# Loading the last third of an image batch in transfers of 16 strided rows

## The chip, the cores and the metric

The kernel runs on one core of a Trainium2 chip. The time is device time in microseconds, the median over runs of the whole kernel; the span of a profile is a little shorter, because it goes from the first to the last instruction. The core's data movers are 16 DMA engines, which work through queues of transfers. "DVE" is VectorE, the engine that does the copies here; "SP" is SyncE, which only issues transfers, and "SPq" is its queue of issued instructions.

## The reference

```python
batch, c, h, w = 32, 3, 256, 256
x = np.random.randn(batch, c, h, w).astype(np.float32)

def reference(x):
    return np.rot90(x, k=2, axes=(-2, -1)).astype(np.float32)
```

Each of the 96 images of 256 x 256 numbers is turned by 180 degrees. Seen as one flat run of 65536 numbers, an image is simply reversed. 25.17 MB are read and 25.17 MB are written.

## The kernel before

The 96 images are worked on in three groups of 32. In a group every image is cut into four strips of E = 16384 numbers, so a group is a tile of 128 rows with 64 KB in each row. All three tiles (A, Bt, Ct) stand in the on-chip memory (SBUF) at once. A group is loaded, VectorE reverses every row in place, and the store writes the four strips of each image in reversed order.

```python
G = 32
E = L // 4            # 16384 numbers, 64 KB
J = E // 8            # 2048
x4 = x.rearrange("b c h w -> (b c) (h w)").rearrange(
    "(g n) (s e) -> g (n s) e", n=G, s=4)
o4 = out.rearrange("b c h w -> (b c) (h w)").rearrange(
    "(g n) (s e) -> g n s e", n=G, s=4)
# ... tiles A, Bt, Ct of 128 x E and T of 128 x J; copy() and back() left out

def load(t, g, lo, hi, queue=nc.sync):
    return queue.dma_start(out=t[:, lo:hi], in_=x4[g][:, lo:hi])

def store(t, g, lo, hi):
    return nc.sync.dma_start(out=o4[g][:, ::-1, lo:hi], in_=t[:, lo:hi])

def inside(t):        # twelve copies: reverse each row in place, through T
    for lo in range(0, E // 2, J):
        hi = E - lo - J
        copy(T[:, :], back(t, hi, hi + J))
        copy(t[:, hi:hi + J], back(t, lo, lo + J))
        copy(t[:, lo:lo + J], T[:, :])

TAIL = 1536
HEAD = 512
load(A, 0, 0, HEAD, nc.scalar)
load(A, 0, HEAD, E)
load(Bt, 1, 0, E)
body = load(Ct, 2, 0, E - TAIL)
load(Ct, 2, E - TAIL, E)
inside(A)
LEAD = 128
store(A, 0, 0, LEAD)
first = store(A, 0, LEAD, E)
tc.add_manual_dep(first.ins, body.ins.name, ...,
    reason="the first store is queued while the last strip is on its way")
for g, t in ((1, Bt), (2, Ct)):
    inside(t)
    store(t, g, 0, E)
```

The third tile comes in two transfers of 128 rows: the first 58 KB of every row (`body`), then the last 6 KB of every row. The large first store is made to wait for `body`: it is issued while the 6 KB pieces are still on their way.

Of the kernel before, what the change touches and what calls it, by code (L numbers as in the profile page):

```python
# [2 lines left out]

os.environ.setdefault("NEURON_RT_ULTRASERVER_MODE", "4")

# [4 lines left out]


@with_exitstack
def kernel(
    ctx: ExitStack,
    tc: tile.TileContext,
    x: bass.AP,
    out: bass.AP,
):

    nc = tc.nc
    P = 128

    B, C, H, W = x.shape
    L = H * W
    G = 32
    E = L // 4
    J = E // 8
# [6 lines that stand above are left out]
    pool = ctx.enter_context(tc.tile_pool(name="slots", bufs=1))  # L42
    A = pool.tile([P, E], x.dtype, tag="A")
    Bt = pool.tile([P, E], x.dtype, tag="B")
    Ct = pool.tile([P, E], x.dtype, tag="C")
    T = pool.tile([P, J], x.dtype, tag="T")

    def back(t, lo, hi):
        return t[:, hi - 1:(lo - 1 if lo else None):-1]

    def copy(dst, src):
        tc.keep_in_program_order(nc.vector.tensor_copy(out=dst, in_=src))  # L52

    def load(t, g, lo, hi, queue=nc.sync):
        return queue.dma_start(out=t[:, lo:hi], in_=x4[g][:, lo:hi])  # L55

    def store(t, g, lo, hi):
        return nc.sync.dma_start(
            out=o4[g][:, ::-1, lo:hi], in_=t[:, lo:hi])

    def inside(t):
# [3 lines that stand above are left out]
            copy(t[:, hi:hi + J], back(t, lo, lo + J))  # L65
            copy(t[:, lo:lo + J], T[:, :])

    TAIL = 1536
    HEAD = 512
    load(A, 0, 0, HEAD, nc.scalar)  # L70
    load(A, 0, HEAD, E)
    load(Bt, 1, 0, E)
    body = load(Ct, 2, 0, E - TAIL)
    load(Ct, 2, E - TAIL, E)
    inside(A)
    LEAD = 128
    store(A, 0, 0, LEAD)
    first = store(A, 0, LEAD, E)
    tc.add_manual_dep(
        first.ins, body.ins.name,  # L80
        mybir.DependencyInfo(mybir.DependencyClass.Sync, mybir.DependencyReason.DATA),
# [6 lines that stand above are left out]
# [1 line left out]
_INS = ['x']  # L89
_OUTS = [((32, 3, 256, 256), 'float32')]  # L90


# [23 lines left out]
```

## Time and profile before

| | |
|---|---|
| time, median of 3 runs | 122.06 us (121.93 to 122.1) |
| span of the profiled run | 120.2 us |
| VectorE busy | 44.2 us, 36 copies of 1.23 us |
| DMA packets on the main queue | 1152, 50.07 MB |
| load of A (its large part), issue to landing | 21.9 us |
| load of Bt, issue to landing | 40.8 us |
| two loads of Ct, issue to landing | 57.9 and 59.3 us |
| store of Bt and of Ct, issue to landing | 39.8 and 42.7 us |

A page of the profile begins with the busy time of each engine. Register, semaphore and DMA-issuing instructions do not count as busy. DMA work has its own lines: packets, bytes, and the share of the 16 engines' span that the packets took. The time from issue to landing includes the time that a transfer stands behind others in its queue. A wait is told as who waited, for whom, the total, the number of times and the longest.

### The profile page before, as it was taken

To read this page: it belongs to the slowest core of one execution; us is meant where nothing else is said; L and a number is where in the kernel's file an instruction comes from. 1 tells how busy PE (TensorE), PEld (TensorE's weight loads), DVE (VectorE), ACT (ScalarE), POOL (GpSimd) and SP (SyncE) were. 2 spreads that over 40 slices of the span, in tenths; PEclk is the share of its full clock that TensorE was granted. 3 is DMA by queue.
4 is the path that set the end of the run, shared out by engine and by line. 5 is a ranking of instruction groups with operands and counts; after the bars stand their busy time and mean duration, and the time that the engine had idled before them with its cause. 6 is when DMAs were issued, how large, how long until landed. Compare 5 with 4: busy or idle time off the path is not lost.

```text
span 120.2 us, 97 instructions
## 1 busy us (share of the span) xinstructions
DVE 44.2 (37%) x36; POOL 0.2 (0%) x4
## 2 busy tenths in 40 slices
DVE  0000000499995099999059999500000000000000
POOL 0000000000000000000000000000000000000000
DMA  9888988899889879979499777988898889888990
GB/s 338 349 349 349 698 349 349 360 654 393 349 349 633 382 316 553 395 316 633 178 452 693 346 346 346 693 349 349 349 698 349 349 349 698 349 349 349 654 393 0
DMA packets 1296, 50.33 MB, mean 419 GB/s; under 512 B 144, under 2 KB 272, under 8 KB 528
## 3 DMA queue, kind: packets, MB, share of 16 engines
q1 hardware_dynamic: 1152, 50.07, 97.0%
q10 hardware_dynamic: 144, 0.26, 0.6%
HBM read 25.17 MB, written 25.17 MB: 419 GB/s over the span
## 4 chain that ended last, share of the span: by engine, by line
DMA 34%; DVE 25%; another core or an unknown queue 4%; issue 1%; SPq 0%; DVEq 0%
DMA Bt<-in_x_dram 34%; DVE T L52 8%; DVE Bt L52 8%; DVE Ct L52 8%; SPq L55 0%; DVEq L52 0%
## 5 line engine op out<-in xcount | busy, mean ns | idle before, releaser
L52 DVE COPY T<-A 128x2048 f32<-128x2048 f32 x4 | 4.9, 1226 | 22.7 <-DMA A<-in_x_dram 22.6
L52 DVE COPY T<-Ct 128x2048 f32<-128x2048 f32 x4 | 4.9, 1227 | 4.5 <-DMA Ct<-in_x_dram 4.4
L52 DVE COPY T<-Bt 128x2048 f32<-128x2048 f32 x4 | 4.9, 1226 | 4.4 <-DMA Bt<-in_x_dram 4.3
L52 DVE COPY Bt<-Bt 128x2048 f32<-128x2048 f32 x4 | 4.9, 1227 | 0.1
L52 DVE COPY A<-A 128x2048 f32<-128x2048 f32 x4 | 4.9, 1227 | 0.1
L52 DVE COPY A<-T 128x2048 f32<-128x2048 f32 x4 | 4.9, 1227 | 0.1
L52 DVE COPY Bt<-T 128x2048 f32<-128x2048 f32 x4 | 4.9, 1227 | 0.1
L52 DVE COPY Ct<-T 128x2048 f32<-128x2048 f32 x4 | 4.9, 1227 | 0.1
L52 DVE COPY Ct<-Ct 128x2048 f32<-128x2048 f32 x4 | 4.9, 1227 | 0.1
L100 POOL MEMSET const-bfloat16-1.0<- 128x1 bf16 x1 | 0.1, 101 | 0.0
L100 POOL MEMSET const-uint8-127<- 128x1 uint8 x1 | 0.1, 101 | 0.0
L100 POOL MEMSET const-float32-0.0<- 128x1 f32 x1 | 0.1, 98 | 0.2 <-issue 0.2
L100 POOL MEMSET const-float32-1.0<- 128x1 f32 x1 | 0.1, 98 | 0.0
## 6 DMA issues: line engine op xcount, KB each, us to landing
out_dram<-A SPq DMA_DIRECT2D x1, 8128.0 KB, 21.1
A<-in_x_dram SPq DMA_DIRECT2D x1, 7936.0 KB, 21.9
Ct<-in_x_dram SPq DMA_DIRECT2D x1, 7424.0 KB, 57.9
Ct<-in_x_dram SPq DMA_DIRECT2D x1, 768.0 KB, 59.3
A<-in_x_dram ACTq DMA_DIRECT2D x1, 256.0 KB, 22.0
out_dram<-A SPq DMA_DIRECT2D x1, 64.0 KB, 35.2
Bt<-in_x_dram SPq DMA_DIRECT2D x1, 40.8
out_dram<-Bt SPq DMA_DIRECT2D x1, 39.8
```

Of the source, the lines that this page charges most:

```text
L52: tc.keep_in_program_order(nc.vector.tensor_copy(out=dst, in_=src))
L100: nc = _bacc.Bacc("TRN2", target_bir_lowering=False, num_devices=1)
```

## The change

The third group is loaded row by row in place of column by column. A transfer takes rows b, b+8, b+16, ..., b+120: sixteen rows of 64 KB. For b = 0 to 6 the rows are whole; for b = 7 they come as the first 16 KB and then the last 48 KB. `body`, for which the first store waits, is now the 16 KB part of the eighth transfer. When it has landed, 48 KB for each of 16 rows are still on their way, as many bytes as in the 6 KB pieces of 128 rows before. The aim is to have fewer and larger pieces of rows, and to leave a single piece per row of the last transfer as the cover for the first store. All loads are also kept in the order in which they stand in the program.

```diff
     def load(t, g, lo, hi, queue=nc.sync):
-        return queue.dma_start(out=t[:, lo:hi], in_=x4[g][:, lo:hi])
+        return tc.keep_in_program_order(
+            queue.dma_start(out=t[:, lo:hi], in_=x4[g][:, lo:hi]))
@@
-    TAIL = 1536
+    TAIL = 12288
+    R = 8
     HEAD = 512
     load(A, 0, 0, HEAD, nc.scalar)
     load(A, 0, HEAD, E)
     load(Bt, 1, 0, E)
-    body = load(Ct, 2, 0, E - TAIL)
-    load(Ct, 2, E - TAIL, E)
+
+    def rows(t, g, b, lo, hi):
+        return tc.keep_in_program_order(nc.sync.dma_start(
+            out=t[b::R, lo:hi], in_=x4[g][b::R, lo:hi]))
+
+    for b in range(R - 1):
+        rows(Ct, 2, b, 0, E)
+    body = rows(Ct, 2, R - 1, 0, E - TAIL)
+    rows(Ct, 2, R - 1, E - TAIL, E)
     inside(A)
     LEAD = 128
     store(A, 0, 0, LEAD)
```

## The prediction

> **What bounds the kernel now.** I read the page's parts 1 to 4 first, then who waited for whom (compute and the DMA queue's own), then a table of busy time in stretches cut at the landings, last the DMA view of one stretch.
>
> ```profile
> DVE 44.2 (37%) x36; POOL 0.2 (0%) x4
> ...
> q1 hardware_dynamic: 1152, 50.07, 97.0%
> ...
> HBM read 25.17 MB, written 25.17 MB: 419 GB/s over the span
> ```
> VectorE works in 37% of the span; the 16 DMA engines have something in hand in 97% of theirs. Every byte is read once and written once, so no byte can be saved: only the rate can change.
>
> ```profile
> DVE T L52 <- DMA A<-in_x_dram: 22.6, 1, 22.6
> DVE T L52 <- DMA Ct<-in_x_dram: 4.4, 1, 4.4
> DVE T L52 <- DMA Bt<-in_x_dram: 4.3, 1, 4.3
> ...
> SPq L58 <- DMA Ct<-in_x_dram: 33.1, 2, 32.5
> ```
> VectorE waits for each of the three loads, so the loads never wait for it. The last line is the wait that the change edits: the queue holds the large first store until the body of the third group has landed.
>
> ```profile
> 22.62 1.23 DVE L52 COPY T<-A 128x2048 f32<-128x2048 f32 x1 [22.62 <-DMA A<-in_x_dram]
> ...
> 42.05 1.23 DVE L52 COPY T<-Bt 128x2048 f32<-128x2048 f32 x1 [4.33 <-DMA Bt<-in_x_dram]
> ...
> 60.27 0.55 SPq L58 DMA_DIRECT2D out_dram<-Bt  x1
> 61.55 1.23 DVE L52 COPY T<-Ct 128x2048 f32<-128x2048 f32 x1 [4.40 <-DMA Ct<-in_x_dram]
> ...
> 76.68 0.54 SPq L58 DMA_DIRECT2D out_dram<-Ct  x1
> ```
> These are rows of the timeline: start, duration, engine. The copies that start a group mark the landings. Group 2 takes 42.05 - 22.62 = 19.43 us, group 3 takes 61.55 - 42.05 = 19.50 us, for 8192 KB = 8.389 MB each: 432 and 430 GB/s, or 27 GB/s for each of 16 engines. A row is 64 KB and an engine carries 8 rows of a group, so a row costs 19.43/8 = 2.43 us.
>
> ```profile
> 42.00:61.50 19.50, 14.72 (x12) 0.00 (x0) 1.00 1.03 438
> 61.50:81.00 19.50, 14.72 (x12) 0.00 (x0) 1.00 0.99 427
> 81.00:100.00 19.00, 0.00 (x0) 0.00 (x0) 1.00 1.02 442
> ```
> Columns: stretch, length, VectorE, GpSimd, clock, DMA share, GB/s. The rate is flat across the turn from loads to stores at 61.5 us. There is no hole at the turn that a better overlap could close.
>
> ```profile
> DMA  0099000980089000990089000990089000499999
> GB/s 0 0 975 975 0 0 0 1584 365 0 0 365 1584 0 0 0 1462 487 0 0 365 1584 0 0 0 1462 487 0 0 365 1584 0 0 0 202 441 403 418 1318 1100
> ```
> This is group 3's stretch, 42.0 to 61.5 us, in slices of 0.49 us. A packet is counted when it ends. A burst comes every five slices, 2.4 us, and lasts about two: the 16 engines finish their rows within about a microsecond of each other. They work in step. From slice 35 on the short 6 KB ends of the rows fill the picture evenly.
>
> [...]
>
> **The change part by part.** Group 3 now arrives as seven transfers of rows b, b+8, ..., b+120 and an eighth in two column parts. Bytes are the same.
>
> 1. Small packets go. Before, each engine carries 8 rows in two pieces, so 8 packets more than with whole rows. Group 3 cost 19.50 us against 19.43 for group 2: these 8 packets are worth 0.07 us. After, an engine has 9 data packets (7 whole, 16 KB, 48 KB), so about 0.06 us comes back.
> 2. Completion messages are added: nine transfers in place of two, seven more completions per engine. The page counts 144 packets under 512 B for 9 transfers, so 7 x 16 = 112 more. If each costs what a cut costs, 0.07/8 = 0.009 us, that is 0.06 us per engine: points 1 and 2 cancel.
> 3. Issuing: the two group-3 loads took 1.01 us of the queue from 1.63 us on, about 0.5 us each. Seven more are 3.5 us, done by about 6.2 us; the DMA engines reach group 3 at 42 us. Nothing.
> 4. The first store's cover. Before, 6 KB x 8 = 48 KB per engine remain when the body has landed; after, 48 KB of one row remain. At 2.43 us per 64 KB both are 1.82 us. The queue issues at 59.6 us, after the body, and the stores follow without a hole. Same cover, no change.
> 5. The ports. [...] All engines go through b in the same order and in step, so at any moment of this load two engines stand at one port[...]. If a port carries what one engine carries, 27 GB/s, a row takes 2 x 2.43 = 4.86 us, and group 3 takes 8 x 4.86 = 38.9 us in place of 19.5: plus 19.4 us. This lies wholly on the path: the stores stand behind these rows in the same engine queues, and VectorE has no other work to offer.
> 6. Given back: an engine that starts its rows a little ahead of its partner has the port alone for that time, and again at the change from b = 3 to b = 4. With engines in step within a microsecond I allow 0.4 us for that.
> 7. VectorE: its work on group 3 starts at about 42 + 38.9 = 81 us and takes 15.1 us (61.55 to 76.68), so ends at 96. The stores of groups 1 and 2 keep the engines till about 81 + 2 x 19.3 = 120, so the third store is queued in time. With half rate the 48 KB cover 3.6 us. Neither binds.
>
> Sum: 122.06 + 19.4 - 0.4 = 141.1 us, with points 1 to 4 at zero.
>
> **The rivals.** (a) The ports do not bind here. Then only points 1 to 4 count and the time is 122.0 to 122.2 us. For it: the trace before cannot tell an engine's limit of 27 GB/s from a port's, and a kernel tuned this far was presumably given this change for a reason. [...] (b) The engines fall out of step. If one of two partners gets the port first each time, it is through b = 0 to 3 at full speed while the other stands; then it goes to the free ports and the other catches up. Group 3 then takes three half groups, 29.2 us, plus 9.7: 131.8 us. Against it: the bursts above show no engine running ahead over 61 us. (c) The HBM pitch binds instead: 16 rows 512 KB apart in place of rows 64 KB apart inside an engine. [...] (d) The 16 rows of a transfer are given to engines by row number, not one each. [...] the time is as in (a). The even count of completions speaks against it only weakly. (e) The queue is late: with many transfers in flight it may have to wait for an early landing before a later issue. It has from 2 to 42 us for it and each further row is 2.4 us of cover, so I give it nothing.
>
> **Range and chances.** I give about three in four to the port mechanism at or near its full size, 138 to 142.5 us; about 8% to partial loss of step, 131 to 138; about 15% to (a), (c) or (d), near 122; the rest to something worse than half rate. A range of 131 to 143 holds the first two. Faster by over 2% would need more than 2.4 us from a kernel whose DMA engines are busy for 97%: 0.02. Within 2%: 0.14. Slower: 0.84.
>
> **What would show it.** Right: the copy that starts group 3 begins near 80.5 us, not 61.5; the stretch from 42 us to it runs at about 215 GB/s with DMA share still near one, since packets take longer and engines do not idle; the bursts come every ten slices' worth, 4.9 us; group 2's landing stays at 42 us and the stores keep 430 GB/s. Rival (b) shows 320 GB/s for a while and full rate in the middle. Wrong altogether: group 3 at 430 GB/s, and the start of its copies still at 61.5 us. A hole between the last load and the first store would show point 4 wrong.

## The result and the profile after

The changed kernel takes 143.44 us (median of 5 runs, 143.19 to 143.55) against 122.04 us for the kernel before beside it: the ratio is 1.175, with a 95% interval of 1.174 to 1.177. The change costs 21.4 us.

The page of the changed kernel, parts 1 and 3:

```profile
DVE 44.2 (31%) x36; POOL 0.2 (0%) x4
...
q1 hardware_dynamic: 1152, 50.07, 97.2%
...
HBM read 25.17 MB, written 25.17 MB: 356 GB/s over the span
```

VectorE does the same 44.2 us of work, and the DMA queue moves the same bytes in the same number of packets (112 fewer pieces of data, 112 more messages of completion). Its share of the engines' time is still 97%, although only 356 GB/s go through in place of 419. So the busy share cannot show this loss: a packet of 64 KB that takes 5.11 us in place of 2.42 counts as busy all the while.

The timeline of the changed kernel, from the landing of group 1 on:

```profile
22.76 1.23 DVE L52 COPY T<-A 128x2048 f32<-128x2048 f32 x1 [22.76 <-DMA A<-in_x_dram]
...
42.66 1.23 DVE L52 COPY T<-Bt 128x2048 f32<-128x2048 f32 x1 [4.80 <-DMA Bt<-in_x_dram]
...
80.21 0.55 SPq L59 DMA_DIRECT2D out_dram<-Bt  x1
83.28 1.23 DVE L52 COPY T<-Ct 128x2048 f32<-128x2048 f32 x1 [25.52 <-DMA out_dram<-A]
...
98.40 0.54 SPq L59 DMA_DIRECT2D out_dram<-Ct  x1
```

Group 3 lands 83.28 - 42.66 = 40.62 us after group 2, in place of 19.50. That is 21.1 us of the 21.4. Group 2 itself lands 0.61 us later than before (42.66 against 42.05); 0.14 us of that is already there when group 1 lands (22.76 against 22.62). The brackets name a store of A as what ended VectorE's wait, but the copy reads Ct. The chain of waits names the right one:

```profile
47.74 35.26 DMA Ct<-in_x_dram
83.00 0.03 DVEq L52
```

The last piece of Ct landed at 47.74 + 35.26 = 83.00 us. The small store of A landed 0.2 us after it (issued at 52.92, 30.3 us to its landing), and the wait was put down to the later of the two.

Stretches of the changed kernel, in the columns of before: the load of group 3, then two stretches of stores.

```profile
42.70:81.00 38.30, 14.68 (x12) 0.00 (x0) 1.00 0.93 192
83.30:102.00 18.70, 14.70 (x12) 0.00 (x0) 1.00 1.03 446
102.60:121.50 18.90, 0.00 (x0) 0.00 (x0) 1.00 1.02 444
```

The stores are as fast as ever. Only the load of group 3 is slow, at less than half rate. From landing to landing it is 8.389 MB / 40.62 us = 207 GB/s; the 192 is lower because packets are counted when they end.

The DMA view from 42.0 to 61.5 us, in slices of 0.49 us as before:

```profile
DMA  0000000999000000069960000000999000000069
GB/s 0 0 0 0 0 0 0 941 672 538 0 0 0 0 0 0 0 134 1076 807 134 0 0 0 0 0 0 0 941 672 538 0 0 0 0 0 0 0 134 1076
```

The bursts now come every ten to eleven slices, 5.1 us, and still all 16 engines are in one burst: each row takes over twice as long (5.11 us in the median, against 2.42 in group 2 of the same run), and the engines stay in step.

The rest of the page gives no second cause. The queue did have to wait before it could issue some of the row transfers, each time for an earlier landing:

```profile
SPq L77 <- DMA Bt<-in_x_dram: 18.5, 1, 18.5
SPq L77 <- DMA A<-in_x_dram: 18.2, 1, 18.2
...
SPq L77 <- DMA Ct<-in_x_dram: 4.6, 1, 4.6
```

But the last of them was issued by 48.3 us, soon after the first row of group 3 had landed, with most of six rows and the 16 KB piece of each engine still ahead of it, so no engine ran dry.

### The profile page after: what moved, and what is told of

The parts are those of the page before. It is cut to its first block, busy times and chain, and to the rows that moved or that the text cites. A ratio compares the mean times of both kernels' runs of the same rounds, so it can differ in the third digit from the quotient of the medians.

```text
span 141.5 us, 109 instructions
## 1 busy us (share of the span) xinstructions
DVE 44.2 (31%) x36; POOL 0.2 (0%) x4
## 3 DMA queue, kind: packets, MB, share of 16 engines
q1 hardware_dynamic: 1152, 50.07, 97.2%
## 4 chain that ended last, share of the span: by engine, by line
DMA 57%; DVE 10%; SPq 1%; issue 0%; DVEq 0%
DMA Ct<-in_x_dram 57%; DVE Ct L52 7%; DVE T L52 4%; SPq L56 1%; DVEq L52 0%
## 5 line engine op out<-in xcount | busy, mean ns | idle before, releaser
L52 DVE COPY T<-Ct 128x2048 f32<-128x2048 f32 x4 | 4.9, 1227 | 25.6 <-DMA out_dram<-A 25.5
## 6 DMA issues: line engine op xcount, KB each, us to landing
out_dram<-A SPq DMA_DIRECT2D x1, 64.0 KB, 30.3
```

## The experiments

Theory P says that two engines which write into one SBUF port share its rate. "Port" is here only a name for whatever the engines share at SBUF: no trace shows a port itself, and which rows lie at one port was assumed; the runs test it by their times. What the runs measure is how long a row takes: 2.42 us in the kernel before, 5.11 us in the changed one. Rival T says that a transfer with few rows per engine is slow in itself. Rival H says that rows 512 KB apart in HBM are slow to read. The table gathers all runs; "group 3" is the time from the copy that starts group 2 to the copy that starts group 3 in each timeline, and each diff is against the changed kernel. From e5 on the diffs show only the lines that are put in.

| run | time, us | ratio to before (95%) | group 3, us |
|---|---|---|---|
| before | 122.04 | | 19.50 |
| changed | 143.44 | 1.174 to 1.177 | 40.62 |
| e1, 16 neighbouring rows | 178.08 (one run) | | 74.03 |
| e2, HBM rows neighbouring | 143.21 | 1.169 to 1.176 | 40.26 |
| e3, 128 rows by columns | 122.60 | 1.003 to 1.005 | 19.98 |
| e4, 32 rows, every fourth | 122.18 | 1.000 to 1.002 | 19.46 |
| e5, halves in turn | 141.44 | 1.156 to 1.161 | 38.86 |
| e6, engines one row apart | 126.17 | 1.030 to 1.037 | 23.69 |
| e7, a store in 16-row transfers | 143.81 | 1.177 to 1.181 | 19.46 |
| e8, halves one after the other | 142.95 | 1.170 to 1.174 | 40.37 |
| e9, changed, other order | 141.89 | 1.162 to 1.165 | 39.43 |
| e10, rows two apart | 143.28 | 1.173 to 1.177 | 40.41 |
| e11, as e1, other order | 179.92 | 1.472 to 1.478 | 75.66 |
| e12, 32 neighbouring rows | 144.24 | 1.179 to 1.183 | 40.47 |

**e1: sixteen neighbouring rows.**

```diff
-            out=t[b::R, lo:hi], in_=x4[g][b::R, lo:hi]))
+            out=t[16 * b:16 * b + 16, lo:hi], in_=x4[g][16 * b:16 * b + 16, lo:hi]))
```

> Sixteen neighbouring rows per transfer in place of every eighth row, all else as changed. Theory P (SBUF ports are shared; a port shared by two engines gives 65.5 KB x 2 in 5.1 us, 25.6 GB/s): [...] a row takes about 10.2 us, group 3 about 82 us, and the kernel 122.0 + 82 - 19.4 = 184 to 185 us. Rival T (a transfer with one row per engine is slow in itself, whatever the rows): no change from the changed kernel, 143 us. Rival H (the HBM pitch of 512 KB makes it slow): the pitch is 64 KB now, so near 122 us.

Its timeline:

```profile
44.05 1.23 DVE L52 COPY T<-Bt 128x2048 f32<-128x2048 f32 x1 [6.08 <-DMA Bt<-in_x_dram]
118.08 1.23 DVE L52 COPY T<-Ct 128x2048 f32<-128x2048 f32 x1 [58.92 <-DMA out_dram<-A]
```

Group 3 takes 74.0 us, 9.25 us a row, or 3.8 times the 2.42 us of a single one. T and H fall: the transfers have the same number and size, the HBM pitch is smaller, and the time grows by 35 us. P has the direction and most of the size, but the row was expected at 10.2 us. If four engines share a port here, as the factor of 3.8 suggests, they get more out of it than two do in the changed kernel: 4 x 65.5 KB / 9.25 us = 28.3 GB/s against 25.6. A part of that comes from the order of the transfers, as e11 will show.

**e2: HBM rows apart from SBUF rows.** The rows of group 3 come out in another order; bytes and work are the same.

```diff
-            out=t[b::R, lo:hi], in_=x4[g][b::R, lo:hi]))
+            out=t[b::R, lo:hi], in_=x4[g][16 * b:16 * b + 16, lo:hi]))
```

> SBUF rows as in the changed kernel (every eighth), but each transfer reads 16 neighbouring rows of HBM; the rows of group 3 come out in another order, with the same bytes and the same work. Theory P: the same as the changed kernel, 143.4 us. Rival H whole: 122 us. Rival H for the part by which a shared row (5.115 us) is longer than two single ones (4.84 us): rows fall to 4.84 us and the kernel to about 141.3 us.

Its timeline:

```profile
42.48 1.23 DVE L52 COPY T<-Bt 128x2048 f32<-128x2048 f32 x1 [4.69 <-DMA Bt<-in_x_dram]
...
82.74 1.23 DVE L52 COPY T<-Ct 128x2048 f32<-128x2048 f32 x1 [25.15 <-DMA out_dram<-A]
```

143.21 us: the rows read from HBM are not the cause, not even of the part above twice a single row. At most it holds 0.05 us a row (40.62 - 40.26 over 8).

**e3: as many transfers, all rows in each.**

```diff
-    for b in range(R - 1):
-        rows(Ct, 2, b, 0, E)
-    body = rows(Ct, 2, R - 1, 0, E - TAIL)
-    rows(Ct, 2, R - 1, E - TAIL, E)
+    W = E // R
+    for b in range(R - 1):
+        load(Ct, 2, b * W, (b + 1) * W)
+    body = load(Ct, 2, (R - 1) * W, E - 1536)
+    load(Ct, 2, E - 1536, E)
```

> Nine transfers with nine completions as in the changed kernel, but of 128 rows and 8 KB columns (the last as 2 KB and 6 KB). Theory P: each engine has its own port, so full rate; only 56 more packets per engine at 0.009 us, 0.5 us: 122.5 us. Rival T in the form that the number of transfers and completions costs: 143 us.

122.60 us, as P expected. Nine transfers with nine completions cost next to nothing. 56 more data packets and 7 more completions per engine are worth 0.56 us together, 0.009 us each on average.

**e4 and e12: the same transfers, other rows.** Both use four transfers of 32 rows, the last in two column parts. e4:

```diff
-    TAIL = 12288
-    R = 8
+    TAIL = 6144
+    R = 4
```

e12 has these two lines and also:

```diff
-            out=t[b::R, lo:hi], in_=x4[g][b::R, lo:hi]))
+            out=t[32 * b:32 * b + 32, lo:hi], in_=x4[g][32 * b:32 * b + 32, lo:hi]))
```

> Four transfers of 32 rows (every fourth row), the last with 40 KB and 24 KB columns, so that again 48 KB per engine cover the first store. [...] Theory P with rows dealt by port: each engine has a port of its own, 122.0 us. Theory P with neighbouring rows of a transfer dealt to the same engine: two engines at one port at each step, 143 us. Rival T (cost per transfer): half as many transfers, about 132 us.

> The run with 32-row transfers again (every fourth row: 122.2 us), but each transfer takes 32 neighbouring rows; number, size and pieces of the transfers are the same. Theory P: [...] 143.3 us, as the changed kernel. Rival T (few rows per engine and transfer is what costs): 122.2 us, as with every fourth row.

The timeline of e4:

```profile
42.17 1.23 DVE L52 COPY T<-Bt 128x2048 f32<-128x2048 f32 x1 [4.45 <-DMA Bt<-in_x_dram]
...
61.63 1.23 DVE L52 COPY T<-Ct 128x2048 f32<-128x2048 f32 x1 [4.36 <-DMA Ct<-in_x_dram]
```

The timeline of e12:

```profile
43.72 1.23 DVE L52 COPY T<-Bt 128x2048 f32<-128x2048 f32 x1 [5.38 <-DMA Bt<-in_x_dram]
...
84.19 1.23 DVE L52 COPY T<-Ct 128x2048 f32<-128x2048 f32 x1 [25.38 <-DMA Ct<-in_x_dram]
```

This is the cleanest pair of the study. Number, size and pieces of the transfers are equal; only the rows differ (in HBM too, but in e2 this was worth at most 0.05 us a row). Every fourth row takes 19.46 us, neighbouring rows take 40.47 us. Which rows of SBUF a transfer names decides, not how many. e4 also says something of how the rows are dealt: its rows take 19.46 / 8 = 2.43 us each, so by theory P its 16 engines stand at different ports at each step. Had neighbours in the transfer gone to one engine, the same theory gave 143 us. e12 is 0.9 us above its expectation; its group 2 lands late, at 43.72 us.

**e5 and e6: engines set apart.** Both take every fourth row of one half of SBUF at a time. In e5 all 16 engines are meant to work in one half, then all in the other:

```diff
+    def part(h, r, i0, i1, lo=0, hi=E):
+        a, z = 64 * h + r + 4 * i0, 64 * h + r + 4 * (i1 - 1) + 1
+        return tc.keep_in_program_order(nc.sync.dma_start(
+            out=Ct[a:z:4, lo:hi], in_=x4[2][a:z:4, lo:hi]))
+    for n in range(7):
+        part(n % 2, n // 2, 0, 16)
+    body = part(1, 3, 0, 16, 0, E - TAIL)
+    part(1, 3, 0, 16, E - TAIL, E)
```

e6 gives eight engines a row in advance, so that they are meant to work in one half while the other eight work in the other:

```diff
+    part(1, 3, 0, 8)
+    for n in range(6):
+        part(n % 2, n // 2, 0, 16)
+    body = part(0, 3, 0, 16, 0, E - TAIL)
+    part(0, 3, 0, 16, E - TAIL, E)
+    part(1, 3, 8, 16)
```

> Transfers of 16 rows again, every fourth row of one half of SBUF (rows 0 to 63 or 64 to 127), the halves in turn; HBM pitch 256 KB. [...] Theory P with engines in step: every row is shared as in the changed kernel. At each turn to the other ports an engine that is ahead finds a free port; the changed kernel has one such turn and its row there took 4.88 us in place of 5.115 us, here there are seven turns, so six more times 0.24 us come back: 143.4 - 1.4 = 142.0 us. Rival T: 143.4 us.

> As the run with halves in turn, but an 8-row transfer goes first, which only 8 of the engines take part in, so they are one row ahead and always stand in the other half's ports than their partners; the second 8 rows come last, on the same 8 engines, so these carry 9 rows and the others 7. Theory P: no port is ever shared, a row takes 2.42 us, and the time is that of the kernel before plus one row of imbalance, 122.0 + 2.4 = 124.5 us. If the 8 engines are not those that share ports with the other 8 or the row order differs: 133 to 143 us. Rival T (transfers with one row per engine are slow in themselves): 144 us or more.

The landings of group 2 and group 3 in e5, then in e6:

```profile
42.16 1.23 DVE L52 COPY T<-Bt 128x2048 f32<-128x2048 f32 x1 [4.48 <-DMA Bt<-in_x_dram]
...
81.02 1.23 DVE L52 COPY T<-Ct 128x2048 f32<-128x2048 f32 x1 [23.76 <-DMA out_dram<-A]
```

```profile
42.45 1.23 DVE L52 COPY T<-Bt 128x2048 f32<-128x2048 f32 x1 [4.72 <-DMA Bt<-in_x_dram]
...
66.14 1.23 DVE L52 COPY T<-Ct 128x2048 f32<-128x2048 f32 x1 [8.59 <-DMA out_dram<-A]
```

With half-SBUF transfers as in e5, one row of offset takes 15.3 us away (141.44 to 126.17). Transfers with at most one row per engine ran at close to full rate here, 2.63 to 2.68 us a row in the trace in place of 4.84 in e5, and this ends rival T. Group 3 takes 23.69 us, nine rows of 2.63 us, which fits eight engines that carry nine rows. e6 is 1.7 us above its expectation, since a row takes 2.63 to 2.68 us and not 2.42. What costs a quarter microsecond per row where by theory P no port should be shared wasn't settled; the two sets of engines change sides at about the same time and may overlap there, but that is not shown.

**e7: does it hold for reads of SBUF?** The loads are those of the kernel before, and only the store of group 2 is cut into rows:

```diff
+        if g == 1:
+            for b in range(R):
+                tc.keep_in_program_order(nc.sync.dma_start(
+                    out=o4[g][b // 4::2, 3 - b % 4, :], in_=t[b::R, :]))
+        else:
+            store(t, g, 0, E)
```

> All loads as in the kernel before; the store of group 2 in eight transfers of 16 rows (every eighth). Theory P, if ports bind reads of SBUF as they bind writes: the store of group 2 takes about 40.7 us in place of 19.3, 143.4 us. If ports bind only writes into SBUF: 122.0 us.

Its stretches: the store of group 1, then group 2 in two stretches.

```profile
61.50:81.00 19.50, 14.72 (x12) 0.00 (x0) 1.00 1.12 427
81.00:100.50 19.50, 0.00 (x0) 0.00 (x0) 1.00 0.84 175
100.50:122.00 21.50, 0.00 (x0) 0.00 (x0) 1.00 1.00 235
```

143.81 us. A store from sixteen rows eight apart costs 21.8 us, as the load into such rows does, with nothing changed on the load side. That a shared port is the cause here too is the author's estimate and has no run of its own: these stores also write rows 512 KB apart in HBM, and e2 has tested only reads of HBM.

**e8 to e11: why a shared row is more than twice a single one.** A single row takes 2.42 us in the trace, so a shared one should take 4.84. The changed kernel's rows take 5.11 us, but e5's rows take 4.84. In steady state only one whole row of the changed kernel is shorter, b = 4 with 4.88 us (against 5.11); that fits rows b = 0 to 3 at one set of ports and b = 4 to 7 at another, with a turn between them, but no trace shows the sets. e5 differs in two ways: in the rows that move together (its pairs), and in that every transfer goes to the other half of SBUF than the one before (its turns). These runs part the two. e8 is e5 in another order, e9 the changed kernel in another order, e11 is e1 in another order, and e10 has another step. The four edits, written here as one:

```diff
+    def part(a, step, lo=0, hi=E):        # sixteen rows a, a + step, ...
+        z = a + 15 * step + 1
+        return tc.keep_in_program_order(nc.sync.dma_start(
+            out=Ct[a:z:step, lo:hi], in_=x4[2][a:z:step, lo:hi]))
+    order = (0, 1, 2, 3, 64, 65, 66, 67)         # e8,  step 4
+    order = (0, 4, 1, 5, 2, 6, 3, 7)             # e9,  step 8
+    order = (0, 1, 32, 33, 64, 65, 96, 97)       # e10, step 2
+    order = (0, 32, 16, 48, 64, 96, 80, 112)     # e11, step 1
+    for a in order[:-1]:
+        part(a, step)
+    body = part(order[-1], step, 0, E - TAIL)
+    part(order[-1], step, E - TAIL, E)
```

> The transfers of the run with halves in turn, in another order: all four of the lower half, then all four of the upper. Open is why a row on a shared port takes 5.115 us in the changed kernel and 4.84 us, twice a single row, with halves in turn. Theory Turn (a row is only 2 x 2.42 us when the engine's row before went to other ports, else 0.27 us more): one turn is left of seven, 143.3 us, rows of 5.11 us but the fifth. Theory Pair (it depends on which engines and which rows share a port): pairs as with halves in turn, 141.4 us, rows of 4.84 us.

> The changed kernel's transfers in the order b = 0, 4, 1, 5, 2, 6, 3, 7, so that each row goes to other ports than the one before. Theory Turn: rows of 4.84 us, 141.4 us. Theory Pair: pairs as in the changed kernel, rows of 5.11 us, 143.4 us.

> Sixteen rows two apart: [...] lower half first, then the upper, so one turn. Theory Turn: as the changed kernel, 143.4 us. Theory Pair, in the form that near rows share better (four near rows got 28.3 GB/s out of a port with 16 neighbouring rows, two far ones 25.6): rows of 4.63 to 4.84 us, 139.7 to 141.4 us.

> Sixteen neighbouring rows, [...]. Theory Turn: every second row is longer by 0.27 us or more than the 9.27 us measured there, by 4 x 0.27 = 1.1 us in all or more: 179.2 us or more. Theory Pair: 178.1 us as there.

All four come out on the side of Turn. e8 loses what e5 had gained, with e5's pairs: 142.95 us. e9 gains with the changed kernel's pairs: 141.89 us, though 0.5 us less than expected: its rows take 4.9 us and not 4.84, and why is open. e10, with rows two apart, is not faster: 143.28 us. e11 is 1.8 us over e1 (179.92 against 178.08). The durations of packets in the traces say how (medians; the words on ports are theory P's):

| packet | changed | e9 |
|---|---|---|
| row on the same ports as the row before | 5.11 us | none |
| row after a turn to other ports | 4.88 us | 4.89 to 4.91 us |
| 16 KB of the last row | 1.28 us (no turn) | 1.11 us (turn) |
| 48 KB that follow on the same port | 3.84 us | 3.80 us |

3.84 us for 48 KB is 5.12 us for 64 KB, and the pieces of 40 KB (3.20 us) and 24 KB (1.92 us) in e12 give the same: the excess grows with the bytes, so it is a rate and not a fee per row. Two engines that share get 2 x 65.5 KB / 5.115 us = 25.6 GB/s together, where one alone gets 65.5 KB / 2.418 us = 27.1. A turn gives back 0.2 us in these two runs and 0.27 us in e5, and the 16 KB pieces show most of it at the start of the row. That partners cross at slightly different moments, so that each is alone at its port for a while, fits this but was only argued.

One more reading would be that certain pairs of engines share a path, whatever the rows. Against it: in the kernel before and in e4 all 16 engines work at once, and group 3 takes 19.50 and 19.46 us, 2.43 to 2.44 us a row; the same engines take 40.47 us in e12, where only the rows differ.

## Why the prediction was right and where it was wrong

- **Points 1 and 2, small packets and completions: right.** e3 measures the two together at 0.009 us each, the size taken from the cut of group 3, and e4 lands within 0.2% of before.
- **Point 3, issuing: right in effect.** Issuing was not done by 6.2 us but by 48.3 us, for the queue waited, as rival (e) feared; still the rows were queued in time.
- **Point 4, the cover: right in effect.** The 48 KB did not take 1.82 us but 3.84, the rate of rows of 5.11 us (point 7 has this). The queue had finished with the first store by 80.21 us, 2.8 us before the last of group 3 landed, and the stores run at 444 to 446 GB/s.
- **Point 5, the ports: right that two engines share, wrong in size.** The sharing was the author's estimate, which no trace before had shown; the rows of 5.11 us, e12 against e4 and the offset of e6 fit it. The step that failed is the sentence "If a port carries what one engine carries, 27 GB/s". Two engines that shared moved 25.6 GB/s together. A row is 5.11 us in place of 4.86, eight rows are 2.0 us more, and that is most of the 2.3 us by which 143.44 exceeds 141.1.
- **Point 6, given back: about right.** The first row took 4.70 us in the median and the row after the turn 4.88, together 0.65 us below steady rows; 0.4 was allowed. Against it stands a cost that the sum didn't have: group 2 lands 0.61 us late. 0.14 us of this comes before any row of group 3 is loaded. For the rest the record of packets shows that the data of group 2 end at 41.71 us, 0.15 us later than before, but the last message of completion lands at 42.57 against 41.96. That engines which have already begun group 3 stand at ports where late engines still write group 2 would explain it, and is argued; in e1, with rows of 9.25 us in group 3, the last packet of group 2 took 2.92 us in place of 2.42, and group 2 lands at 44.05 us. With both, 141.1 + 2.0 - 0.25 + 0.6 = 143.45 us. That this meets 143.44 so closely is luck: group 3 took 40.62 us where the terms give 38.9 + 2.0 - 0.65 = 40.25, and what follows its landing is 0.43 us shorter than before (58.22 us of the span against 58.65).
- **Point 7: right.** Neither VectorE nor the cover binds: the third store is issued at 98.40 us, while the engines carry the first.
- **The rivals.** (a), (c) and (d) are out by e12 against e4, by e2, and by the changed kernel itself. (b) did not happen by itself: the bursts stay together. e6 shows what it is worth when it is forced.
- **The range** ended at 143.0 and missed by 0.44 us. It left room below for engines out of step, and almost none above, though the trace before held nothing on how two engines share a port. With half of the 430 GB/s of before, 215, taken as certain for group 3, the sum had no term for the difference to the 207 GB/s measured.

## What to carry to other kernels

A DMA transfer is not described by its bytes and its count of rows: which rows of SBUF move at the same moment decides too. In these runs the 8.389 MB of group 3 came at 420 GB/s by columns of all 128 rows (e3) and at 431 by every fourth row of all 128, 32 rows at a time (e4); but at 207 by sixteen rows eight apart (changed) and by 32 neighbours (e12), at 208 by sixteen rows two apart (e10), at 216 by every fourth row of one half of SBUF (e5), and at 113 by 16 neighbours (e1). If a tile must be cut, try the first two ways: e3 and e4 cost at most 0.6 us, the cut by every eighth row 21.4. A full busy share of the DMA engines beside a fallen GB/s is the sign to look for: 97.2% at 356 GB/s here, against 97.0% at 419 before, and in e7's stores a share of 1.00 at 235 GB/s against 427 for the store of group 1.

## What the runs showed of the hardware that was not expected

In the words of theory P, two engines that stay at one port from row to row move 25.6 GB/s together (rows of 5.115 us), less than the 27.1 of one alone, while four move 27.2: in e11 a row on the same ports as the row before takes 9.64 us, and 4 x 65.5 KB / 9.64 us is 27.2 GB/s. Why two do worse than one or four is open; no run tried three, and pieces of 16 to 48 KB gave a pair the same rate as whole rows. And the order of row transfers alone, with the same collisions, is worth 1.5 us (e8 against e5, 142.95 and 141.44, and the changed kernel against e9, 143.44 and 141.89).
